# Last expert product of a two-block transformer: activations stationary, 512 table columns streaming

## The chip, the cores and the metric

One Trainium2 chip, one of its cores. The metric is the time of one execution on the device in microseconds (us); the kernel before took 1345.21 us, the median of three runs (1343.98 to 1345.67).

## The reference, cut to what matters

Two transformer blocks run one after the other on 256 tokens of width 1024, in float32. Only the end of the second block is touched:

```python
gate2 = (silu(c) @ w_ada + b_ada)[5 * 1024:]          # one value per channel
h2 = rms_norm(x, g_norm2) * (1 + scale2) + shift2
# peer: 8 heads pick 16 of 16384 experts each, per token
act = gelu(einsum('td,tkd->tk', h2, expert_u[idx]))
y = einsum('tk,tkd->td', g * act, expert_v[idx])       # expert_v: 16384 x 1024
out = x + gate2 * y
```

The kernel does not gather. It multiplies with all 16384 rows of both tables and uses a dense matrix X (16384 experts by 256 tokens) that is zero where an expert was not picked. The last product is y = X^T V, with V = `expert_v`: 256 x 16384 times 16384 x 1024.

## The kernel before, in words

**Products in three passes.** Float32 values are cut in two fp32r parts, high and low (`hilo`, L389: ScalarE copies the high part, VectorE subtracts to get the low part). `mm3` (L262) makes one product of three matmuls, high by high (L265), high by low (L266), low by high (L267), with the first operand pair stationary in TensorE and the second one streaming. Each matmul carries its own weight load.

**Table units.** All weights come in units of 128 x 1024 floats (512 KB). `Units` (L136) keeps five raw buffers ahead by DMA on SyncE's queue, and cuts a unit two ahead of its use: ScalarE writes `whi` (L127), VectorE writes `wlo` (L170), three buffers each. `units.get()` returns the pair and starts the cut of the unit two further on.

**The stage before.** 128 units of the first expert table are multiplied with the normed activations; the results, masked and weighted, lie in `xs0` (128 x 96 x 256 floats, unit i in column block i) and `xs1` (units 96 to 127).

**The stage of the change** (L1417 to the end). `yacc` is four PSUM banks of 128 x 512 floats (`big4`, L288). For each of 128 units i, `w_cut(i)` (L1387) cuts X(i), 128 experts x 256 tokens, in two fp32r parts `wx`, made two units ahead, in buffers of three units, two buffers. `v_unit(i)` (L1393) then takes the eight blocks of 128 table columns in turn: the table block is stationary, the 256 tokens stream. So one unit has 8 x 3 = 24 matmuls of 256 columns, and the sum lies with the 1024 channels on the partitions: bank n//2 holds blocks n and n+1, 256 tokens each. Beside it, eight rows of `w_ada` (`ad`, 512 KB each) are loaded and reduced on VectorE (L1430): they give gate2 as `mod[:, 40:48]`, channels on the partitions. The residual x was stored to DRAM earlier (`hsave`, L1141, channels on the partitions) and is loaded back to `hx` (L1436).

**The end.** Units 126 and 127 are done block by block, both units for block 0, then for block 1 and so on, so that blocks finish one after the other (L1437 to 1440). For each block one VectorE instruction (L1442) computes yacc * gate2 + hx, and five DMAs store the result, the last two of 128 KB.

**What sets the order.** The text is a program for a framework that plans the order of each engine's queue when the kernel is built: an instruction whose inputs are there in the plan's own clock can be placed ahead of earlier text, instructions earlier in the text go first where several are ready. It sets all semaphores from the reads and writes of tiles; in PSUM two accesses to one bank are put in order even where their columns differ. On the chip every queue runs in its planned order.

**A stage with the other operand order** exists in the kernel: `proj_tok` (L431) has token activations stationary and 512 columns of the cut table unit streaming, 12 matmuls of 512 columns per unit, for `v`, `mv`, `sv` and `mlv`.

Of the kernel before, what the change touches and what calls it, by code (L numbers as in the profile page):

```python
# [8 lines left out]
F32 = mybir.dt.float32  # L9
# [4 lines left out]
AF = mybir.ActivationFunctionType  # L14
OP = mybir.AluOpType
AX = mybir.AxisListType

T = 256
# [89 lines left out]
def body(tc, nc, a, out):  # L108
    ctx = ExitStack()
    with ctx:  # L110
        _body(ctx, tc, nc, a, out)


def _body(ctx, tc, nc, a, out):
    V, S, G, PE = nc.vector, nc.scalar, nc.gpsimd, nc.tensor
    cst = ctx.enter_context(tc.tile_pool(name="cst", bufs=1))
    wp = ctx.enter_context(tc.tile_pool(name="wp", bufs=1))
    xp = ctx.enter_context(tc.tile_pool(name="xp", bufs=1))
# [7 lines left out]
    def act(o, i, f, **k):  # L126
        return S.activation(o, i, f, **k)  # L127

    def load(t, src):
        nc.sync.dma_start(t, src)  # L130
        return t
# [53 lines left out]
    units = Units([a["w"][u] for u in range(NU)] + [a["eu"][i] for i in range(128)] + [a["ev"][i] for i in range(128)])  # L185
# [9 lines left out]
    bada = cst.tile([128, 48], F32, name="bada")  # L195
# [34 lines left out]
    def C(name):  # L230
        if name in made:
            return made[name]
        lo, hi = CN[name]
        return cn[:, lo:hi] if hi <= NC1 else cn2[:, lo - NC1:hi - NC1]

    def P_(name, i=None):
        lo, hi = SM[name]
        return sm[:, lo:hi] if i is None else sm[:, lo + i:lo + i + 1]
# [23 lines left out]
    def mm3(o, w, x, start, stop):  # L262

        (wh, wl), (xh, xl) = w, x
        PE.matmul(o, wh, xh, start=start, stop=False, skip_group_check=True)  # L265
        PE.matmul(o, wh, xl, start=False, stop=False, skip_group_check=True)  # L266
        last[0] = PE.matmul(o, wl, xh, start=False, stop=stop, skip_group_check=True).ins  # L267

    def mm(o, w, x, start, stop):
        return PE.matmul(o, w, x, start=start, stop=stop, skip_group_check=True)  # L270

    def pst(tag, shape, bufs):
        return ps.tile(shape, F32, name=tag, tag=tag, bufs=bufs)
# [4 lines left out]
    def p_ax(shape=(128, 512)):  # L278
        return pst("ax", list(shape), 4)
# [4 lines left out]
    def p_first(i, n=T):  # L284

        return (p_acc() if i % 4 < 2 else p_mm())[:, :n]

    def big4():  # L288
        return [p_acc(), p_acc(), p_mm(), p_mm()]
# [4 lines left out]
    o_ = p_ax()  # L294
# [15 lines left out]
    mod = cst.tile([128, 48], F32, name="mod")  # L310
    mraw = cst.tile([128, 48], F32, name="mraw")
# [38 lines left out]
    def rstd(ssum, r):  # L350

        n = r.shape[-1]
        r0 = mp.tile([128, n], F32, name="r0", bufs=2)
        t = mp.tile([128, n], F32, name="rt", bufs=2)
        act(r0, ssum, AF.Ln, bias=epsc)
        act(r0, r0, AF.Exp, scale=-0.5)
        act(t, r0, AF.Square, scale=math.sqrt(0.5))
        V.scalar_tensor_tensor(t, ssum, EPS, t, op0=OP.add, op1=OP.mult)
        V.scalar_tensor_tensor(r, t, 1.5, r0, op0=OP.subtract, op1=OP.mult, reverse0=True)

    class Norm:
# [14 lines left out]
        def finish(self):  # L376
            p = p_ax((128, T))
            tc.keep_in_program_order(mm(p, C("o1024"), self.acc, True, True))
            self.r = mp.tile([128, T], F32, name="rstd", bufs=2)
            rstd(p, self.r)  # L380
# [40 lines left out]
    def proj_T(kind, i, x, o=None, n=T):  # L421
        w = unit(kind, i)
        o = p_mm()[:, :n] if o is None else o
        for c in range(8):
            s = slice(c * 128, (c + 1) * 128)
            mm3(o, (w[0][:, s], w[1][:, s]), (x[0][:, c], x[1][:, c]), c == 0, c == 7)
            if c == 4:
                tick()
        return o
# [32 lines left out]
    def gate_rows(w, mh, x):  # L462

        o = p_mm()[:, :T]
        m = w.shape[2]
        for c in range(8):
            mm(o[0:m], w[:, c], x[0][:, c], c == 0, False)
            mm(o[0:mh], w[:, c, 0:mh], x[1][:, c], False, c == 7)
        return o
# [133 lines left out]
    o = og[0]  # L603
# [52 lines left out]
    for i in range(4):  # L656
        o = proj_T("q", i, xn)
        NL.add(headnorm(o, C("b64"), [(gq[:, 0:1], qn[:, i])], r=n1.r))
        utick()
        o = proj_T("k", i, xn)  # L660
# [36 lines left out]
    for g in (3, 2, 1, 0):  # L697
        o = proj_T("p", g, xn)
# [98 lines left out]
    for i in range(4):  # L797
        o = proj_T("mq", i, xn, p_first(i))
# [83 lines left out]
    t = b2.tile([128, 128], F32, name="below")  # L882
# [59 lines left out]
    for n in range(8):  # L942
        i = n // 2
        outs = [(None, ks[:, i])] if n % 2 else [(gq[:, 2 + j:3 + j], qs[:, 2 * i + j]) for j in range(2)]
        kind = "sk" if n % 2 else "sq"
        if n < NXA:
            o = proj_T(kind, i, xa, p_first(n, T + 2), n=T + 2)
# [4 lines left out]
            while qo and n >= 1:  # L952
                m, o, outs = qo.pop(0)
# [5 lines left out]
        else:  # L959
            o = proj_T(kind, i, xn)  # L960
# [5 lines left out]
    o = gate_rows(wgi, 36, xn)  # L966
# [57 lines left out]
    for i in range(8):  # L1024
        o = proj_T("ml", i, xn)
        b = cpad[i % 2]
        act(b[:, 4:], o, AF.Copy)
        w = [P_("conv_w", 4 * i + j) for j in range(4)]
# [65 lines left out]
    for i in range(4):  # L1094
        o = proj_T("mlo", i, xn)
# [45 lines left out]
    hsave = dr.tile([128, 8, T], F32, name="hsave")  # L1141
# [7 lines left out]
    xs0 = pp_.tile([128, 96, T], F32, name="xs0")  # L1149
    scr = pp_.tile([128, 8192], F32, name="scr", tag="xs1")  # L1150
    scr_u = scr.bitcast(U32)
    o_ = [0]
# [230 lines left out]
    yacc = None  # L1383
    wsp = {}
    wx = [None]

    def w_cut(i):  # L1387
        if i % 3 == 0:
            wx[0] = pp_.tile([128, 3, 2, T], F32R, name="wx", tag="oh", bufs=2)
        wsp[i] = (wx[0][:, i % 3, 0], wx[0][:, i % 3, 1])  # L1390
        hilo(X(i), *wsp[i])

    def v_unit(i):  # L1393
        w = units.get()
        x = wsp.pop(i)
        for n in range(8):
            s = slice(n * 128, (n + 1) * 128)
            mm3(yacc[n // 2][:, (n % 2) * T:(n % 2 + 1) * T], (w[0][:, s], w[1][:, s]), x,
                i == 0 and n % 2 == 0, False)

    gr_ = [0]
    for i in range(128):
# [14 lines left out]
    yacc = big4()  # L1417
# [2 lines left out]

    ad = xp.tile([128, 2, 1024], F32, name="ad", tag="xl")
    load(ad[:, 0], crep_src)
    for i in range(126):
        w_cut(i + 2)
        if i % 12 == 0 and i < 96:
            load(ad[:, 1], a["ada"][40 + i // 12])
        if i % 12 == 8 and i < 96:
            j = 40 + i // 12
            jk = xp.tile([128, 1024], BF, name="jk", tag="xh", bufs=1)
            V.scalar_tensor_tensor(jk, ad[:, 1], 1.0, ad[:, 0], op0=OP.mult, op1=OP.mult, accum_out=mraw[:, j:j + 1])  # L1430
        v_unit(i)
    V.tensor_tensor(mod[:, 40:48], mraw[:, 40:48], bada[:, 40:48], op=OP.add)
    ws = [units.get() for _ in range(2)]
    xs = [wsp.pop(126 + k) for k in range(2)]
    hx = xp.tile([128, 8, T], F32, name="hx", tag="xh", bufs=1)
    load(hx, hsave)  # L1436
    for n in range(8):  # L1437
        s = slice(n * 128, (n + 1) * 128)
        for k, w in enumerate(ws):
            mm3(yacc[n // 2][:, (n % 2) * T:(n % 2 + 1) * T], (w[0][:, s], w[1][:, s]), xs[k], False, k == 1)  # L1440
    for n in range(8):
        V.scalar_tensor_tensor(hx[:, n], yacc[n // 2][:, (n % 2) * T:(n % 2 + 1) * T], mod[:, 40 + n:41 + n], hx[:, n],  # L1442
                               op0=OP.mult, op1=OP.add)
        if n % 2 and n < 6:
            nc.sync.dma_start(out[:, n - 1:n + 1], hx[:, n - 1:n + 1])
        elif n > 5:
            nc.sync.dma_start(out[:, n:n + 1], hx[:, n:n + 1])

# [98 lines left out]
```

## Time and profile before

| what | value |
|---|---|
| median of 3 runs | 1345.21 us |
| profiled execution | 1344.46 us, span 1342.7 us |
| granted TensorE clock, mean | 0.998 of 2.4 GHz |
| TensorE busy | 1331.0 us, 99% of the span, 10821 matmuls |
| VectorE, ScalarE, GpSimd busy | 1006.3, 771.3, 85.5 us |
| DMA | 251.98 MB, mean 188 GB/s |
| the stage of the change | 970.1 us to the end |

The busy time of a matmul is longer than its distance to the next one, since matmuls overlap in the array; what counts is the distance from start to start. Starts are in us from the start of the span.

### The profile page before, as it was taken

The numbers are of one execution on the slowest core, as the hardware profiler recorded it, in microseconds if no ns is written. First come the engines' busy times: TensorE is split into PE (matmuls) and PEld (weight loads), VectorE is DVE, ScalarE is ACT, GpSimd is POOL, SyncE is SP. The second block draws the span as 40 slices with busy tenths as digits, with TensorE's granted clock in tenths as the row PEclk, the third lists the DMA queues.
The fourth block names the chain that finished last, engine by engine and source line by source line (L and its number), as shares of the span: only waits on it lengthen the run. The fifth ranks groups of instructions, "written<-read, shape, count | busy, mean of one in ns | idle before, by whom it ended". The sixth has DMA issues, their size and how long they took to land.

```text
span 1342.7 us, 27108 instructions
## 1 busy us (share of the span) xinstructions
PE 1331.0 (99%) x10821; PEld 1292.2 (96%) x10821; DVE 1006.3 (75%) x1930; ACT 771.3 (57%) x1430; POOL 85.5 (6%) x71
## 2 busy tenths in 40 slices
PE   9999999999999999999999999999999999999998
PEld 7889899999998899999999999999999999999998
DVE  7977698887798789799978888985576555555554
ACT  8757664444588887544756665554444444444442
POOL 0301010000100001086000000000000000000000
PEclk9999999999999999999999999999999999999999
DMA  7535469988543335655555555546687565565553
GB/s 280 179 109 187 143 201 330 327 301 271 161 139 123 126 109 166 216 181 191 172 180 158 158 158 158 158 157 179 190 288 246 183 188 178 184 185 179 186 187 97
DMA packets 70000, 251.98 MB, mean 188 GB/s; under 512 B 7777, under 2 KB 8689, under 8 KB 69489
## 3 DMA queue, kind: packets, MB, share of 16 engines
q1 hardware_dynamic: 69872, 250.24, 57.7%
q8 instruction: 85, 1.39, 0.4%
q14 instruction: 43, 0.34, 0.1%
HBM read 248.11 MB, written 2.10 MB: 186 GB/s over the span
## 4 chain that ended last, share of the span: by engine, by line
PE 95%; DVE 3%; issue 1%; ACT 0%; DMA 0%; DVEq 0%; SPq 0%; ACTq 0%
PE mm L265 18%; PE mm L266 18%; PE mm L267 18%; PE ax L270 9%; PE acc L266 8%; PE acc L265 8%; PE acc L267 8%; PE ax L267 3%; PE ax L266 3%; PE ax L265 3%; DVE wlo L170 1%; DVE xnl L751 1%; DVE xal L751 1%; DVE h L761 1%; PE mm L270 0%
## 5 line engine op out<-in xcount | busy, mean ns | idle before, releaser
L127 ACT ACTIVATE whi<-raw 128x1024 fp32r<-128x1024 f32 (+1 forms) x415 | 438.0, 1056 | 438.5 <-PE mm L266 323.3
L170 DVE TENSOR_TENSOR wlo<-raw,whi 128x1024 fp32r<-128x1024 f32 x392 | 479.1, 1223 | 263.4 <-ACT whi L127 260.8
L265 PE MATMUL mm<-xnh,whi 128*128 128x256 f32 x1304 | 375.2, 288 | 0.0
L267 PE MATMUL mm<-xnh,wlo 128*128 128x256 f32 x1304 | 369.1, 283 | 0.0
L266 PE MATMUL mm<-xnl,whi 128*128 128x256 f32 x1304 | 369.0, 283 | 0.0
L265 PEld LDWEIGHTS mm<-xnh,whi 128*128 128x128 f32 x1304 | 249.7, 191 | 0.9 <-issue 0.3
L266 PEld LDWEIGHTS mm<-xnl,whi 128*128 128x128 f32 x1304 | 250.0, 192 | 0.5
L267 PEld LDWEIGHTS mm<-xnh,wlo 128*128 128x128 f32 x1304 | 249.8, 192 | 0.1
L265 PE MATMUL mm<-wx,whi 128*128 128x256 f32 x512 | 144.9, 283 | 0.0
L266 PE MATMUL acc<-wx,whi 128*128 128x256 f32 x512 | 144.9, 283 | 0.0
L267 PE MATMUL mm<-wx,wlo 128*128 128x256 f32 x512 | 144.9, 283 | 0.0
L265 PE MATMUL acc<-wx,whi 128*128 128x256 f32 x512 | 144.9, 283 | 0.0
L267 PE MATMUL acc<-wx,wlo 128*128 128x256 f32 x512 | 144.9, 283 | 0.0
L266 PE MATMUL mm<-wx,whi 128*128 128x256 f32 x512 | 144.9, 283 | 0.0
L266 PE MATMUL ax<-xnl,whi 128*128 128x256 f32 x352 | 100.1, 284 | 1.5 <-DVE xnl L751 1.5
L267 PE MATMUL ax<-xnh,wlo 128*128 128x256 f32 x352 | 99.7, 283 | 0.4 <-DVE wlo L170 0.4
L265 PE MATMUL ax<-xnh,whi 128*128 128x256 f32 x352 | 99.7, 283 | 0.0
L267 PEld LDWEIGHTS acc<-wx,wlo 128*128 128x128 f32 x512 | 98.3, 192 | 0.0
L265 PEld LDWEIGHTS acc<-wx,whi 128*128 128x128 f32 x512 | 98.3, 192 | 0.0
L266 PEld LDWEIGHTS acc<-wx,whi 128*128 128x128 f32 x512 | 98.3, 192 | 0.0
L265 PEld LDWEIGHTS mm<-wx,whi 128*128 128x128 f32 x512 | 98.3, 192 | 0.0
L266 PEld LDWEIGHTS mm<-wx,whi 128*128 128x128 f32 x512 | 98.3, 192 | 0.0
(380 smaller groups left out, 2504.2 us busy)
## 6 DMA issues: line engine op xcount, KB each, us to landing
raw<-in_w_dram SPq DMA_DIRECT2D x157, 512.0 KB, 4.2
raw<-in_eu_dram SPq DMA_DIRECT2D x128, 512.0 KB, 3.6
raw<-in_ev_dram SPq DMA_DIRECT2D x128, 512.0 KB, 3.9
ada<-in_ada_dram SPq DMA_DIRECT2D x40, 512.0 KB, 5.0
ad<-in_ada_dram SPq DMA_DIRECT2D x8, 512.0 KB, 4.3
h<-in_xT_dram SPq DMA_DIRECT2D x4, 256.0 KB, 5.1
memT<-in_memT_dram SPq DMA_DIRECT2D x1, 1024.0 KB, 6.3
hsave<-h SPq DMA_DIRECT2D x1, 1024.0 KB
```

The source lines that it names most:

```text
L127: return S.activation(o, i, f, **k)
L170: i = e.tensor_tensor(lo, r, hi.bitcast(F32), op=OP.subtract)
L265: PE.matmul(o, wh, xh, start=start, stop=False, skip_group_check=True)
L266: PE.matmul(o, wh, xl, start=False, stop=False, skip_group_check=True)
L267: last[0] = PE.matmul(o, wl, xh, start=False, stop=stop, skip_group_check=True).ins
L270: return PE.matmul(o, w, x, start=start, stop=stop, skip_group_check=True)
L751: V.scalar_tensor_tensor(x[1][:, c, :T], h[:, c], g[:, c:c + 1], x[0][:, c, :T].bitcast(F32), op0=OP.mult, op1=OP.subtract)
L761: V.tensor_tensor(h[:, c], o[:, n * T:(n + 1) * T], h[:, c], op=OP.add)
```

## The change

The last product swaps its operands. The cut activations `wx` are stationary (128 experts x 128 tokens), 512 columns of the table unit stream. One unit has then 4 x 3 = 12 matmuls of 512 columns; bank b holds tokens 128u to 128u+127 on the partitions (u = b // 2) and channels 512n to 512n+511 (n = b % 2). With tokens on the partitions, three things are added. The residual, stored with channels on the partitions, is loaded earlier into the used-up columns 0 to 7 of `xs0`, turned by 16 TensorE transposes of 128 x 128 (`h_turn`, four calls), and copied by ScalarE to columns 8 to 15. The gate must lie along the free axis in every partition: `g_row` (two calls) makes 8 diagonal matrices on VectorE (identity times gate column) and multiplies a matrix of ones with them (one float32 matmul of 512 columns per call), and ScalarE copies the result to `grow`. The end multiplies with `grow` and adds `hT`: two VectorE instructions in place of one. Bank 3 is finished in two halves of 256 columns. The output tensor changes its layout to tokens on partitions; the host turns it back.

```diff
-    def v_unit(i):
-        w = units.get()
-        x = wsp.pop(i)
-        for n in range(8):
-            s = slice(n * 128, (n + 1) * 128)
-            mm3(yacc[n // 2][:, (n % 2) * T:(n % 2 + 1) * T], (w[0][:, s], w[1][:, s]), x,
-                i == 0 and n % 2 == 0, False)
+    def v_unit(i, parts=range(4), start=False, stop=False, w=None, x=None):
+
+        w = units.get() if w is None else w
+        x = wsp.pop(i) if x is None else x
+        for b in parts:
+            u, n = divmod(b, 2)
+            us, s = slice(128 * u, 128 * u + 128), slice(512 * n, 512 * n + 512)
+            mm3(yacc[b], (x[0][:, us], x[1][:, us]), (w[0][:, s], w[1][:, s]), start, stop)
...
+    hx = xs0[:, 0:8]
+    hT = xs0[:, 8:16].rearrange("p a t -> p (a t)").rearrange("p (u d) -> p u d", u=2)
+    gd = xs0[:, 16:20].rearrange("p a t -> p (a t)").rearrange("p (c n) -> p c n", c=8)
+    grow = xs0[:, 20:24].rearrange("p a t -> p (a t)")
+    ones = xs0[:, 24, 0:128]
+
+    def h_turn(k):
+        u, n = divmod(k, 2)
+        p = p_ax()
+        for c in range(4):
+            PE.transpose(p[:, c * 128:(c + 1) * 128], hx[:, 4 * n + c, u * 128:(u + 1) * 128], C("ident"))
+        act(hT[:, u, n * 512:(n + 1) * 512], p, AF.Copy)
+
+    def g_row(n):
+        for c in range(4 * n, 4 * n + 4):
+            V.tensor_scalar(gd[:, c], C("ident"), mod[:, 40 + c:41 + c], None, op0=OP.mult)
+        p = p_ax()
+        mm(p, ones, gd[:, 4 * n:4 * n + 4].rearrange("p c n -> p (c n)"), True, True)
+        act(grow[:, n * 512:(n + 1) * 512], p, AF.Copy)
+
     for i in range(126):
...
-        v_unit(i)
-    V.tensor_tensor(mod[:, 40:48], mraw[:, 40:48], bada[:, 40:48], op=OP.add)
+        v_unit(i, start=i == 0)
+        if i == 30:
+            load(hx, hsave)
+            G.memset(ones, 1.0)
+        if 40 <= i < 56 and i % 4 == 0:
+            h_turn((i - 40) // 4)
+        if i == 98:
+            V.tensor_tensor(mod[:, 40:48], mraw[:, 40:48], bada[:, 40:48], op=OP.add)
+        if i in (102, 106):
+            g_row((i - 102) // 4)
     ws = [units.get() for _ in range(2)]
     xs = [wsp.pop(126 + k) for k in range(2)]
-    hx = xp.tile([128, 8, T], F32, name="hx", tag="xh", bufs=1)
-    load(hx, hsave)
-    for n in range(8):
-        s = slice(n * 128, (n + 1) * 128)
-        for k, w in enumerate(ws):
-            mm3(yacc[n // 2][:, (n % 2) * T:(n % 2 + 1) * T], (w[0][:, s], w[1][:, s]), xs[k], False, k == 1)
-    for n in range(8):
-        V.scalar_tensor_tensor(hx[:, n], yacc[n // 2][:, (n % 2) * T:(n % 2 + 1) * T], mod[:, 40 + n:41 + n], hx[:, n],
-                               op0=OP.mult, op1=OP.add)
...
+    def finish(b, s):
+        u, n = divmod(b, 2)
+        ds = slice(512 * n + s.start, 512 * n + s.stop)
+        V.tensor_tensor(o_[:, b, s], yacc[b][:, s], grow[:, ds], op=OP.mult)
+        V.tensor_tensor(o_[:, b, s], o_[:, b, s], hT[:, u, ds], op=OP.add)
+        nc.sync.dma_start(out[:, u, ds], o_[:, b, s])
+
+    for b in range(3):
+        for k in range(2):
+            v_unit(126 + k, (b,), stop=k == 1, w=ws[k], x=xs[k])
+        finish(b, slice(0, 512))
+    for s in (slice(0, 256), slice(256, 512)):
+        for k in range(2):
+            mm3(yacc[3][:, s], (xs[k][0][:, 128:], xs[k][1][:, 128:]),
+                (ws[k][0][:, 512 + s.start:512 + s.stop], ws[k][1][:, 512 + s.start:512 + s.stop]), False, k == 1)
+        finish(3, s)
```

## Rows read from the trace of the kernel before

**Rows 1.** The profile's page: the span, busy time by engine.

```profile
span 1342.7 us, 27108 instructions
PE 1331.0 (99%) x10821; PEld 1292.2 (96%) x10821; DVE 1006.3 (75%) x1930; ACT 771.3 (57%) x1430; POOL 85.5 (6%) x71
```

**Rows 2.** Busy time in two stretches: us, busy (count) by engine, clock, DMA.

```profile
970.00:1020.00 50.00, 50.00 (x419) 50.00 (x419) 35.11 (x50) 23.77 (x34) 0.00 (x0) 1.00 0.84 277
1050.00:1100.00 50.00, 50.00 (x419) 50.00 (x418) 27.08 (x36) 22.84 (x33) 0.00 (x0) 1.00 0.59 182
```

**Rows 3.** Waits from 970 to 1333: total us, times, longest.

```profile
ACT whi L127 <- PE mm L266: 191.6, 126, 1.8
DVE wlo L170 <- ACT whi L127: 150.7, 116, 1.7
```

**Rows 4.** Timeline of one table unit: start us, us, engine, line.

```profile
1312.79 0.28 PE L265 MATMUL acc<-wx,whi 128*128 128x256 f32 x1
...
1312.87 1.06 ACT L127 ACTIVATE whi<-raw 128x1024 fp32r<-128x1024 f32 x1 [1.82 <-PE mm L266]
...
1313.96 1.23 DVE L170 TENSOR_TENSOR wlo<-raw,whi 128x1024 fp32r<-128x1024 f32 x1 [1.66 <-ACT whi L127]
...
1315.67 0.28 PE L265 MATMUL acc<-wx,whi 128*128 128x256 f32 x1
```

**Rows 5.** Timeline, 512-column matmuls: 12 steps in `v`, then 12 in `mv`.

```profile
13.93 0.39 PE L265 MATMUL acc<-whi,xnh 128*128 128x512 f32 x1
...
16.65 0.39 PE L265 MATMUL acc<-whi,xnh 128*128 128x512 f32 x1
...
137.09 0.40 PE L265 MATMUL acc<-whi,mnh 128*128 128x512 f32 x1
...
139.90 0.39 PE L265 MATMUL acc<-whi,mnh 128*128 128x512 f32 x1
```

**Rows 6.** Timeline: transposes (L525 to L528), then a float32 product (L270).

```profile
63.69 0.27 PE L525 MATMUL ax<-cn,p 128*128 128x128 f32 x1
...
64.23 0.27 PE L528 MATMUL ax<-cn,p 128*128 128x128 f32 x1
64.34 0.60 PE L270 MATMUL ax<-sqacc,o 128*128 128x256 f32 x2
...
64.90 0.28 PE L266 MATMUL mm<-xnl,whi 128*128 128x256 f32 x1
```

**Rows 7.** Two groups of VectorE instructions: busy us, mean ns.

```profile
L842 DVE TENSOR_TENSOR sgu<-ax,rstd 128x512 f32<-128x512 f32 x22 | 15.1, 688 | 7.2 <-PE ax L267 7.1
L391 DVE TENSOR_TENSOR wx<-xs,wx 128x256 fp32r<-128x256 f32 x128 | 46.4, 417 | 0.0
```

**Rows 8.** Instructions of L1432 and L1430, and of tile hx: counts, starts.

```profile
L1432 DVE TENSOR_TENSOR mod<-mraw,bada x1: 159/159/159, 1018.9 to 1018.9; 128x8 f32<-128x8 f32 x1
L1430 DVE SCALAR_TENSOR_TENSOR jk<-ad x8: 1216/1226/1228, 977.6 to 1016.6; 128x1024 bf16<-128x1024 f32 x8
L130 SPq DMA_DIRECT2D hx<-hsave x1: 327/327/327, 1017.9 to 1017.9; - x1
DMA to landing us min/median/max: 2.1/3.1/6.6
```

**Rows 9.** Tile raw, 970 to 1030, its landings.

```profile
DMA to landing us min/median/max: 3.5/4.6/7.0
```

**Rows 10.** Timeline of the end: blocks 0 and 1, and the last block.

```profile
1334.27 0.28 PE L267 MATMUL acc<-wx,wlo 128*128 128x256 f32 x1
...
1334.59 0.87 DVE L1442 SCALAR_TENSOR_TENSOR hx<-acc,mod,hx 128x256 f32<-128x256 f32 x2 [2.13 <-PE acc L267]
...
1338.59 0.28 PE L267 MATMUL mm<-wx,wlo 128*128 128x256 f32 x1
1338.91 0.88 DVE L1442 SCALAR_TENSOR_TENSOR hx<-mm,mod,hx 128x256 f32<-128x256 f32 x2 [0.56 <-PE mm L267]
1339.42 0.81 SPq L1447 DMA_DIRECT2D out_dram<-hx  x2
```

More of the change, by code (lines that the diff above doesn't have):

```diff
@@ L1430, in _body @@
             V.scalar_tensor_tensor(jk, ad[:, 1], 1.0, ad[:, 0], op0=OP.mult, op1=OP.mult, accum_out=mraw[:, j:j + 1])
-        v_unit(i)
-    V.tensor_tensor(mod[:, 40:48], mraw[:, 40:48], bada[:, 40:48], op=OP.add)
+        v_unit(i, start=i == 0)
[8 more added lines that the diff above has]
+            g_row((i - 102) // 4)
     ws = [units.get() for _ in range(2)]
     xs = [wsp.pop(126 + k) for k in range(2)]
-    hx = xp.tile([128, 8, T], F32, name="hx", tag="xh", bufs=1)
-    load(hx, hsave)
-    for n in range(8):
-        s = slice(n * 128, (n + 1) * 128)
-        for k, w in enumerate(ws):
-            mm3(yacc[n // 2][:, (n % 2) * T:(n % 2 + 1) * T], (w[0][:, s], w[1][:, s]), xs[k], False, k == 1)
-    for n in range(8):
-        V.scalar_tensor_tensor(hx[:, n], yacc[n // 2][:, (n % 2) * T:(n % 2 + 1) * T], mod[:, 40 + n:41 + n], hx[:, n],
-                               op0=OP.mult, op1=OP.add)
[L1444 to L1447, printed above, removed]
+    o_ = xs0[:, 32:40].rearrange("p a t -> p (a t)").rearrange("p (b d) -> p b d", b=4)
+    def finish(b, s):
[13 more added lines that the diff above has]
+        finish(3, s)
 def _cols(w, n0):
@@ L1542 @@
         aps[n] = nc.dram_tensor(f"in_{n}_dram", v.shape, mybir.dt.from_np(v.dtype), kind="ExternalInput").ap()
-    out = nc.dram_tensor("out_dram", (128, 8, T), F32, kind="ExternalOutput").ap()
+    out = nc.dram_tensor("out_dram", (128, 2, 1024), F32, kind="ExternalOutput").ap()
     with tile.TileContext(nc) as tc:
@@ L1547 @@
     o = r.results[0]["out_dram"]
-    return np.ascontiguousarray(o.transpose(2, 1, 0).reshape(1, T, 1024))
+    return np.ascontiguousarray(o.transpose(1, 0, 2).reshape(1, T, 1024))
```

## The prediction

> **What bounds the kernel now.** The page first [rows 1]: TensorE is busy for 99% of the span, VectorE for 75%, ScalarE for 57%. A busy TensorE proves little, because matmuls overlap, so I look next at the stage of the change by itself. There TensorE has no hole at all: 50.00 us busy in 50, at the full clock (2.4 GHz), with DMA at 0.84 of its time in the first 50 us and 0.59 later [rows 2]. The waits say the same from the other side: ScalarE waits for TensorE 126 times (whi waits for the last reader of its buffer), VectorE waits for ScalarE, and no row has TensorE waiting [rows 3]. So the stage lasts as long as TensorE needs for its matmuls, from start to start. One unit runs from 1312.79 to 1315.67 [rows 4]: 2.88 us for 24 matmuls, 0.120 us each. At 2.4 GHz 256 columns alone are 0.1067 us; some 13 ns per matmul come on top.
>
> **The change part by part.**
>
> *The operand swap.* A unit has 12 matmuls of 512 columns in place of 24 of 256. The same columns stream, so the gain lies only in what comes on top of them. The kernel already runs this form in `proj_tok`: twelve steps from 13.93 to 16.65 are 2.72 us, 0.2267 us each [rows 5], and 512 columns alone are 0.2133, so again some 13 ns on top. The count is halved and the extra is not doubled: 2.88 - 2.72 = 0.16 us per unit, for 126 units 20.2 us. There is a worse row: in `mv` twelve steps take 137.09 to 139.90 = 2.81 us, 0.234 each, which would leave 0.07 per unit, 8.8 us. I take 0.2267, since the `v` rows come from a long unbroken run over unit borders, beside the same cuts on ScalarE and VectorE, and the changed stage is the longest unbroken run of all; `mv` goes in bursts of some 15 matmuls. I keep 0.234 for the range. The half as many weight loads give nothing more than that: a load is hidden in either row.
>
> The Trainium skill speaks against this gain ("TensorE: Matmul & The Clock Gate", section "Back-to-back issue gap"): the isolated gap is N/2.4 + 2.5 ns, which would be an estimated 109.2 and 215.8 ns here, and the swap would save 31 ns per unit, 3.9 us in all, less than what is added below. The trace has 120.0 and 226.7 ns, so by the rows the extra is five times larger, and with it the gain.
>
> *What must keep up with the shorter unit.* The cut of a unit starts 0.08 us after a unit's start (1312.87) and ends at 1313.96 + 1.23 = 1315.19, 2.4 us after it [rows 4]; it is for a unit two further on, that is 5.44 us after with the new length. 3.0 us of slack stay. ScalarE's and VectorE's work per 50 us is 22.8 and 27.1 us [rows 2]; a unit 6% shorter does not fill them. Raw data: five buffers, so 5 x 2.72 = 13.6 us per turn; less the 2.4 us of the cut some 11 us are left for a landing of 7.0 at worst [rows 9]. At 512 KB per 2.72 us DMA moves 193 GB/s, and the trace has 277 [rows 2]. Cost nothing; were a landing late by its worst 7.0 us, the slack of 3.0 us would leave 4 us per event.
>
> *Residual and gate, in the middle of the stage.* The 16 transposes stand in TensorE's queue. From 63.69 to 64.23 five steps take 0.54 us, 0.108 each [rows 6]: 1.7 us. The two gate products are plain float32; such a product of 256 columns runs as two passes, and from 64.34 to 64.90, less 0.12 us for the fp32r matmul in between, it takes 0.44 us [rows 6]. For 512 columns I double it: 0.88, 1.8 us for both. As bounds, 0.23 each if it ran like the fp32r rows (1.3 less), and twice 0.88 above (1.8 more). After each of six interruptions some matmuls may start at `mv`'s spacing (7 ns more); ten each make 0.4 us, I take 0.3.
> The load of the residual (1 MB), the memset, the new column of `mod`, 8 diagonal products and 6 ScalarE copies leave TensorE's path if the queues put them early. They will: `mod` stood after the loop in the text and ran at 1018.9, right after the last reduction (1016.6), 320 us ahead of its use, and the residual's load ran at 1017.9 [rows 8]. So when TensorE comes to `g_row` the diagonals have long been made, and I cost that wait at nothing. In text order VectorE would do four diagonals (each between the 159 ns of `mod` and the 417 of 256 columns [rows 7, 8]) behind a wlo, and TensorE with all the units behind it would stand for up to 1.1 us, twice. The load is moved past SyncE's queue of raw loads: it takes up to 6.6 us to land [rows 8], as it did before in the same stretch, and no wait came of it [rows 3]. If the first transpose is placed before the landing, TensorE stands up to 6.6 us; if the new uses of `xs0` make ScalarE's cut of `wx` wait for the load, 6.6 - 3.0 = 3.6 us are seen. I take 0 for both, because 30 and 40 units of text lie between, and keep 6.6 for the range.
>
> *The end.* I count from the start of units 126 and 127. Before: the last of 48 matmuls starts at 47 x 0.12 = 5.64, VectorE comes 0.32 later and needs 0.88 for the two blocks of the bank [rows 10], so 6.84 us to the last store's issue. The first bank is read at 1334.59, 0.32 after the last matmul of its second block (1334.27), though its first block was done six matmuls earlier: a bank is read only when all its matmuls are done. After: six matmuls per bank, last starts at 1.13, 2.49, 3.85; VectorE is ready 0.43 later (0.32 and 0.11 for the longer matmul). A finish is two instructions of 512 columns, 0.688 each [rows 7], 1.38 us, a little more than the 1.36 that TensorE needs per bank: VectorE is busy 1.56 to 5.70 without a break. Half A of bank 3 has its last matmul at 4.7, but its product waits for VectorE: 5.70 to 6.12. Half B lies in the same bank, so TensorE stands from 4.8 to some 6.2; its last matmul starts at 6.8, VectorE comes at 7.14 and takes 2 x 0.417: 7.97. The store is of 128 KB as before. Cost 1.1 us. Bounds: 0.3 gain if no bank wait and no backlog existed (24 x 0.2267 = 5.44 against 5.76), 2.0 cost if each handover took 0.3 us more.
>
> *The sum*: -20.2 + 1.7 + 1.8 + 0.3 + 1.1 = -15.3 us. The profiled execution took 1344.46 us (span 1342.7), which gives 1329.2; it lies 0.75 under the median of 1345.21. Against the median: 1329.9 us.
>
> **The rivals.** 0.2%, 2.7 us, is about what a measurement can tell from no change.
>
> *A. The 512-column matmul stays at `mv`'s spacing.* 8.8 gained, 4.9 paid: 1341.3 us. For it: in `mv` it held over whole bursts; against it: 12 matmuls in 2.72 us in `v` [rows 5].
>
> *B. The new work is placed where TensorE meets it.* Load not landed (6.6), or both diagonals late (2.2), on top of the forecast: 1332 to 1337 us. Against it: everything that could go early in the old trace did [rows 8].
>
> *C. Slower: the extra per matmul grows with the width.* Place: all 126 units. At 0.240 us, twice 0.120, nothing is gained and 4.9 us are paid: 1350.1 us. It decides from (2.88 - 4.9/126)/12 = 0.2368 us on. For it: `mv` at 0.234 has gone more than half the way from 0.2267 to 0.240, and is 3 ns short of the break-even; against it, the `v` rows. The skill's isolated gaps above would end on the same side, an estimated 1346.
>
> *D. No change to be told*, some A with some B: 1343 to 1347.
>
> **How the numbers follow.** Forecast with its own uncertain sizes (1327 to 1333): 0.76. A: 0.09. B: 0.07. C: 0.04. D: 0.04. Faster: 0.76 + 0.09 + 0.07 = 0.92; same 0.04; slower 0.04. Below, the bounds give an end with 0.3 gained in place of 1.1 paid and gate products 1.3 cheaper, 2.7 us under the forecast: 1327. Above, the range takes in B up to a stall of 6 us and the part of A that settles half-way: 1336. Outside lie some 0.15.
>
> **What would show it.** In the changed profile one unit lasts 2.72 us, 12 matmuls 0.227 apart; 2.76 or more says A or C. The stage lasts some 353 us where it lasted 369, and what comes before it is as long as now. The 16 transposes and two gate products fill 3.5 us of TensorE, without a wait for VectorE or DMA in front of them; a wait there is B. The copies' ScalarE time and the diagonals cause no wait of TensorE. At the end TensorE waits about 1.4 us for VectorE between the two halves of the last bank, and VectorE runs through the first three finishes without a break. The forecast is wrong if the units' spacing is over 0.230, if a hole of over 1 us stands in the stage before its end, or if the stages ahead of it change length by over 2 us.

## The result and the profile after

The changed kernel takes 1329.19 us (median of four runs, 1329.14 to 1330.08), the kernel before 1344.99 on the same chip (1343.98 to 1345.67): a ratio of 0.9885, 95% interval 0.9868 to 0.9902. That is 15.8 us less. Forecast were 15.3 less and 1329.9 us, with a range of 1327 to 1336. The profiled execution took 1329.14 us with a span of 1327.4, at a mean granted clock of 0.998.

The page of after, against [rows 1]: TensorE still fills 99% of a shorter span, with 1510 matmuls fewer, and its weight loads fall from 96 to 91%.

```profile
span 1327.4 us, 24145 instructions
PE 1313.2 (99%) x9311; PEld 1212.8 (91%) x9311; DVE 1010.4 (76%) x1940; ACT 775.0 (58%) x1436; POOL 85.7 (6%) x72
```

The two stretches of [rows 2] after the change (us, busy time and count of each engine, clock, DMA share, GB/s):

```profile
970.00:1020.00 50.00, 50.00 (x225) 41.52 (x224) 35.67 (x50) 24.15 (x35) 0.00 (x0) 1.00 0.85 297
1050.00:1100.00 50.00, 50.00 (x226) 41.38 (x225) 28.10 (x36) 25.66 (x39) 0.00 (x0) 1.00 0.57 190
```

TensorE is busy throughout at the full clock, as before, and now loads weights for 41.5 us of 50 where it loaded for 50.0. The other engines have the same work and the same room.

The waits from 970 to 1327, against [rows 3] (total us, times, longest):

```profile
...
ACT whi L127 <- PE mm L267: 170.6, 125, 2.1
DVE wlo L170 <- ACT whi L127: 132.5, 114, 2.4
...
DVE xs L1471 <- PE acc L267: 1.8, 1, 1.8
...
PE mm L265 <- DVE xs L1471: 0.5, 1, 0.5
```

ScalarE and VectorE still wait for TensorE. TensorE itself waits once, 0.5 us, and that is at the end.

A table unit after the change, from the timeline of TensorE (start us, us, engine, line), against [rows 4, 5]:

```profile
1199.74 0.39 PE L265 MATMUL mm<-whi,wx 128*128 128x512 f32 x1
...
1202.46 0.39 PE L265 MATMUL mm<-whi,wx 128*128 128x512 f32 x1
```

Twelve steps lie between the two rows: 2.72 us, 0.2267 each. From the start of its first `wx` matmul to that of its last, the stage takes 352.67 us (970.64 to 1323.32) where it took 368.52 (970.07 to 1338.59), and 4.04 us follow to the end of the span where 4.10 followed: together 15.91 less. Two more profiles of the changed kernel gave 352.67 and 352.67. What lies ahead of the stage is not touched, and its length differs from run to run (968.7 to 971.4 over all the runs shown here); so lengths of this stage are compared below beside the times.

### The profile page after: what moved, and what is told of

The parts are those of the page before. It is cut to its first block, busy times and chain, and to the rows that moved or that the text cites. A ratio compares the mean times of both kernels' runs of the same rounds, so it can differ in the third digit from the quotient of the medians.

```text
span 1327.4 us, 24145 instructions
## 1 busy us (share of the span) xinstructions
PE 1313.2 (99%) x9311; PEld 1212.8 (91%) x9311; DVE 1010.4 (76%) x1940; ACT 775.0 (58%) x1436; POOL 85.7 (6%) x72
## 4 chain that ended last, share of the span: by engine, by line
PE 95%; DVE 3%; issue 1%; DMA 1%; ACT 0%; SPq 0%; ACTq 0%; DVEq 0%
PE mm L265 18%; PE mm L266 18%; PE mm L267 18%; PE ax L270 9%; PE acc L266 7%; PE acc L265 7%; PE acc L267 7%; PE ax L267 3%; PE ax L266 3%; PE ax L265 3%; DVE wlo L170 1%; DVE xnl L751 1%; DVE xal L751 1%; DVE h L761 1%; DMA raw<-in_w_dram 1%
## 5 line engine op out<-in xcount | busy, mean ns | idle before, releaser
L267 PE MATMUL mm<-xnh,wlo 128*128 128x256 f32 x1304 | 369.1, 283 | 0.0
L267 PEld LDWEIGHTS mm<-xnh,wlo 128*128 128x128 f32 x1304 | 249.8, 192 | 0.1
L265 PE MATMUL acc<-whi,wx 128*128 128x512 f32 x256 | 100.8, 394 | 0.0
L265 PE MATMUL mm<-whi,wx 128*128 128x512 f32 (+1 forms) x258 | 100.1, 388 | 0.5 <-DVE xs L1471 0.5
L267 PE MATMUL ax<-xnh,wlo 128*128 128x256 f32 x352 | 99.7, 283 | 0.4 <-DVE wlo L170 0.4
L267 PE MATMUL mm<-whi,wx 128*128 128x512 f32 (+1 forms) x258 | 100.0, 387 | 0.0
L266 PE MATMUL mm<-wlo,wx 128*128 128x512 f32 (+1 forms) x258 | 100.0, 387 | 0.0
L267 PE MATMUL acc<-whi,wx 128*128 128x512 f32 x256 | 99.7, 389 | 0.0
L266 PE MATMUL acc<-wlo,wx 128*128 128x512 f32 x256 | 99.6, 389 | 0.0
L266 PEld LDWEIGHTS ax<-xnl,whi 128*128 128x128 f32 x352 | 67.4, 192 | 2.6 <-DVE xnl L751 2.5
L267 PEld LDWEIGHTS ax<-xnh,wlo 128*128 128x128 f32 x352 | 67.5, 192 | 0.6 <-DVE wlo L170 0.6
L265 PEld LDWEIGHTS ax<-xnh,whi 128*128 128x128 f32 x352 | 67.5, 192 | 0.0
L265 PEld LDWEIGHTS mm<-whi,wx 128*128 128x128 f32 x258 | 48.4, 188 | 10.7 <-DVE xs L1471 0.7
L266 PEld LDWEIGHTS mm<-wlo,wx 128*128 128x128 f32 x258 | 48.4, 188 | 10.0
```

## The experiments

"Stage" is the length just defined. The column of differences compares it with the 352.67 of the changed kernel, which three profiles gave. The stage is that of the one profiled execution. The time is a median, except for e2, e3, e4, e6 and e7, which were run once. e1 to e4 ran on a chip where the kernel before took 1345.73 us.

| run | what | time, us | stage, us | difference |
|---|---|---|---|---|
| after | the change | 1329.19 | 352.67 | |
| r_after, r_after2 | the same again | 1328.99, 1329.06 | 352.67, 352.67 | 0 |
| e1_swap256 | swapped, 256 columns | 1348.91 | 372.69 | +20.02 |
| e2_swap128 | swapped, 128 columns | 2158.93 | | |
| e3_no_extra | no turning, no gate products | 1325.57 | 348.91 | -3.76 |
| e4_whole_bank | last bank not split | 1328.77 | 351.72 | -0.95 |
| e5_gate_dma | gate through DRAM | 1329.09 | 352.13 | -0.54 |
| e6_late_diag | diagonals late | 1329.58 | 353.36 | +0.69 |
| e7_late_load | residual's load late | 1329.49 | 353.22 | +0.55 |
| e8_no_pe | turning and gate off TensorE | 1326.81 | 349.60 | -3.07 |
| e9_spread | e8, its transfers spread | 1326.34 | 355.12 | +2.45 |
| e10_rows | e9, gate stored as rows | 1325.96 | 349.07 | -3.60 |

### e1_swap256: the operand order or the width?

The operands stay swapped, but each matmul streams 256 columns.

```diff
-            mm3(yacc[b], (x[0][:, us], x[1][:, us]), (w[0][:, s], w[1][:, s]), start, stop)
+            for q in range(2):
+                qs, ws_ = slice(256 * q, 256 * q + 256), slice(512 * n + 256 * q, 512 * n + 256 * q + 256)
+                mm3(yacc[b][:, qs], (x[0][:, us], x[1][:, us]), (w[0][:, ws_], w[1][:, ws_]), start and q == 0, stop)
```

> The operands stay swapped (activations stationary, table columns streaming), but each unit streams 24 times 256 columns in place of 12 times 512. Theory (the gain is the halved number of matmuls, each with some 13 ns on top of its columns, whichever operand is stationary): 0.120 us per matmul, 2.88 per unit, the gain of 20.2 us is gone and the additions stay: about 1349.4 us, slower than before by 4.5. Rival (the gain comes from having the activations stationary, whose four 128 x 128 blocks serve the whole unit, and not from the width): 2.72 us per unit, about 1329.

1348.91 us (1347.36 to 1349.89), ratio to before 1.0022, 95% interval 1.0012 to 1.0031. In the timeline of TensorE three steps take 0.36 us:

```profile
1199.80 0.28 PE L267 MATMUL mm<-whi,wx 128*128 128x256 f32 x1
...
1200.16 0.28 PE L267 MATMUL mm<-whi,wx 128*128 128x256 f32 x1
```

So 0.120 us each, as in [rows 4] with the other operand order. The stage is 20.02 us longer than with 512 columns. So the theory holds: the gain lies in the width, and with it in half as many matmuls and weight loads. Which operand is stationary makes no difference at 256 columns, and without the width the change is a loss of 0.2%.

### e2_swap128: what comes on top at 128 columns?

As e1, with four matmuls of 128 columns.

> As the changed kernel, but 48 matmuls of 128 columns per unit. Theory in its plain form (13.4 ns on top of 128 columns at 2.4 GHz, 53.3 ns): 0.0667 us each, 3.20 per unit, 126 x 0.48 = 60 us more than the changed kernel, about 1390. Rival (the weight load of a 128 x 128 fp32r block can't be hidden under fewer than some 256 columns, so that a floor near the 0.108 us of the 128-column transposes in the trace of before sets the spacing): 48 x 0.108 = 5.2 us per unit, 310 us more, about 1640.

2158.93 us, far from either number. Ahead of its first stall, in the timeline of TensorE, seven steps take 0.78 us:

```profile
979.84 0.28 PE L266 MATMUL mm<-wlo,wx 128*128 128x128 f32 x1
...
980.62 0.27 PE L267 MATMUL mm<-whi,wx 128*128 128x128 f32 x1
```

That is 0.111 us, 58 ns above the 53 of the columns; at 256 and at 512 it was 13. So a second limit holds at 128 columns, just under the 0.120 of 256. This is the rival's spacing (0.108) and not the theory's (0.067); that the weight load sets it, as the rival has it, the run does not show. At 0.111 a unit needs 5.3 us. The rest of the time is in the busy time by stretch (same columns as above):

```profile
960.00:985.00 25.00, 25.00 (x220) 25.00 (x219) 11.06 (x15) 8.06 (x12) 0.00 (x0) 1.00 0.54 188
985.00:1012.00 27.00, 20.09 (x127) 19.77 (x126) 9.94 (x17) 4.09 (x6) 0.00 (x0) 0.70 0.49 162
1012.00:1050.00 38.00, 38.00 (x180) 38.00 (x180) 8.21 (x11) 4.09 (x6) 0.00 (x0) 0.50 0.31 106
1050.00:1377.00 327.00, 327.00 (x1535) 327.00 (x1535) 51.83 (x73) 43.91 (x65) 0.21 (x1) 0.50 0.16 52
...
2050.00:2150.00 100.00, 100.00 (x898) 100.00 (x898) 28.29 (x35) 22.29 (x31) 0.00 (x0) 1.00 0.21 71
```

TensorE waited 6.9 us of the 27 from 985 on (for `wlo`, up to 4.1 us at a time), the granted clock fell to 0.50 (1.2 GHz), and it stayed there until about 2020 us although TensorE was busy without a break from 1012 on. At 0.50 a matmul takes 327/1535 = 0.213 us, twice 0.107. The timeline of TensorE before and at the rise:

```profile
2015.68 0.41 PE L267 MATMUL mm<-whi,wx 128*128 128x128 f32 x1
2015.89 2.02 PE L270 MATMUL ax<-xs 128*128 128x512 f32 x2
2016.92 1.09 PE L265 MATMUL acc<-whi,wx 128*128 128x128 f32 x1
...
2019.30 0.40 PE L267 MATMUL acc<-whi,wx 128*128 128x128 f32 x1
2019.52 0.30 PE L265 MATMUL acc<-whi,wx 128*128 128x128 f32 x1
2019.66 0.27 PE L266 MATMUL acc<-wlo,wx 128*128 128x128 f32 x1
```

The run answers its question by the rows at full clock alone; the total says nothing of the change.

### e3_no_extra: the price of the added work on TensorE

```diff
-        p = p_ax()
-        for c in range(4):
-            PE.transpose(p[:, c * 128:(c + 1) * 128], hx[:, 4 * n + c, u * 128:(u + 1) * 128], C("ident"))
-        act(hT[:, u, n * 512:(n + 1) * 512], p, AF.Copy)
+        act(hT[:, u, n * 512:(n + 1) * 512].rearrange("p (c t) -> p c t", c=4), hx[:, 4 * n:4 * n + 4, u * 128:(u + 1) * 128], AF.Copy)
...
-        p = p_ax()
-        mm(p, ones, gd[:, 4 * n:4 * n + 4].rearrange("p c n -> p (c n)"), True, True)
-        act(grow[:, n * 512:(n + 1) * 512], p, AF.Copy)
+        act(grow[:, n * 512:(n + 1) * 512], gd[:, 4 * n:4 * n + 4].rearrange("p c n -> p (c n)"), AF.Copy)
```

> The 16 transposes and the two gate products are left out (ScalarE copies the unturned residual and the diagonals in their place, so the output lacks the right residual and gate). Theory: TensorE saves 1.77 and 1.73 us, which no other work hides: 3.5 us less than the changed kernel, about 1325.7. Rival (they stood beside a limit elsewhere, the cut or the DMA): about 1329.

1325.57 us, stage 3.76 us shorter, close to the theory's 3.5. The timeline of after shows the parts, first one call of `h_turn`, then one of `g_row`:

```profile
1081.96 0.39 PE L267 MATMUL mm<-whi,wx 128*128 128x512 f32 x1
1082.20 0.60 PE L1436 MATMUL ax<-cn,xs 128*128 128x128 f32 x4
...
1083.10 0.40 PE L267 MATMUL acc<-whi,wx 128*128 128x512 f32 x1
...
1252.55 0.39 PE L267 MATMUL mm<-whi,wx 128*128 128x512 f32 x1
1252.78 1.02 PE L270 MATMUL ax<-xs 128*128 128x512 f32 x2
...
1254.11 0.40 PE L267 MATMUL acc<-whi,wx 128*128 128x512 f32 x1
```

Each pair of L267 rows is three matmuls apart, 0.68 us if nothing lay between. The first pair has 1.14: 0.44 for four transposes (0.109 each) and some 20 ns of restart. The second has 1.56: a little under 0.88 for the two passes of the float32 product. Times four and two: 1.8 and 1.7 us, and the rest of the 3.76, 0.2 to 0.3, goes in the main to the matmuls after the interruptions, some of which start up to 9 ns wider apart than 227.

### e4_whole_bank: is the split of the last bank worth its stall?

```diff
-    for b in range(3):
+    for b in range(4):
...
-    for s in (slice(0, 256), slice(256, 512)):
...
-        finish(3, s)
```

> The last bank is finished as one piece of 512 columns, not in two halves: no matmul waits for the read of its bank. Theory (the split costs TensorE a stall of 0.7 us, and gives back a shorter last product and a store of half the size): VectorE ends some 0.3 us earlier, the last store is of 256 KB and lands some 1 us later than one of 128 KB: 0.7 us more, about 1329.9, hard to tell from the changed kernel in the time, plain in the trace. Rival (the split only costs): 0.7 us less, about 1328.5.

1328.77 us. The stage is 0.95 us shorter, since TensorE no longer stops, but 5.09 us follow it where 4.04 did, because the last product, addition and store are twice as large: 356.81 against 356.71 in all. By this sum the two expectations (0.7 us more, 0.7 us less) missed by 0.6 and 0.8 us. The split costs as much as it gives.

### r_after, e5_gate_dma, e7_late_load, e8_no_pe

These four ran on one chip. The first is the changed kernel again, 1328.99 us (ratio to before 0.9879, interval 0.9863 to 0.9896).

> The changed kernel once more, beside the two next ones on the same chip: 1329.2 us as before, ratio 0.988 to 0.989.

e5_gate_dma brings the gate to all partitions through DRAM instead of by diagonals and TensorE:

```diff
-        for c in range(4 * n, 4 * n + 4):
-            V.tensor_scalar(gd[:, c], C("ident"), mod[:, 40 + c:41 + c], None, op0=OP.mult)
...
+        if n == 0:
+            gsave = dr.tile([8, 128], F32, name="gsave")
+            nc.sync.dma_start(gsave.rearrange("a b -> b a"), mod[:, 40:48])
+            load(grow, gsave.rearrange("a b -> (a b)")[None, :].to_broadcast([128, 1024]))
```

> The gate row goes through DRAM: one store of 128 x 8 values in turned order and one load that repeats the 1024 values in all partitions, in place of the diagonals, the ones and the two float32 products. Theory (TensorE's time is the stage's time, DMA and SyncE have room): 1.73 us less than the changed kernel, about 1327.4. Rival (the store of single values, 1024 of 4 bytes, or the load of 512 KB delays a raw table unit beyond the 3 us of slack): no gain or some us more, with a wait of ScalarE for DMA in the trace.

1329.09 us (1328.52 to 1329.46), ratio 0.988, interval 0.9864 to 0.9897: nothing gained, as the rival had it. The two products are gone (1.7 us), but the stage is only 0.54 us shorter. Its waits from 990 to 1320 show why:

```profile
ACT whi L127 <- DMA raw<-in_ev_dram: 7.3, 2, 5.9
```

So do its landings of `raw` there, from issue to landing:

```profile
DMA to landing us min/median/max: 3.3/3.5/13.8
```

In after no ScalarE row names a DMA, and the worst landing of that stretch is 5.2. Two matmuls of TensorE start 1.26 us apart at 1038.56, some 1.0 more than the rule. The queue of SyncE shows the store of the gate at 1022.38, one raw load at 1023.52 and the next only at 1032.93, behind the gate's load at 1032.52, which had to wait for the store. Two causes were possible here: the wait in the queue, or the store itself.

e7_late_load holds the residual's load back to unit 40 of the text, close to its use:

```diff
-            load(hx, hsave)
...
+        if i == 40:
+            with tc.issue_after(last_load[0]):
+                load(hx, hsave)
```

> The residual's load is held back in SyncE's queue behind the raw load that stands last in the text at unit 40, and the first turn follows the same unit: the cover of the early load is taken away. Theory (TensorE's queue is planned with a guess of the landing; if the guess is early, TensorE stands for the rest): a hole of 1 to 5 us in front of the first transposes, and as much on the time, 1330 to 1334. Rival (the plan moves the transposes far enough back): no hole, 1329.2.

1329.49 us, stage 0.55 us longer. The first transpose waits for the load:

```profile
1083.29 0.63 PE L1436 MATMUL ax<-cn,xs 128*128 128x128 f32 x4 [0.31 <-DMA xs<-hsave]
```

The load was issued at 1076.7 (982.1 in after) and took 6.5 us, and TensorE came to the transpose some 6 us after the issue, because the plan also moved the transpose back by four matmuls. Neither expectation holds: there is a hole, but the theory's 1 to 5 us were too many. A late landing costs only what exceeds the time between issue and use.

e8_no_pe takes both jobs off TensorE: VectorE transposes blocks of 32 x 32, 16 DMAs of 64 KB move the blocks between partitions, and the gate goes as in e5.

```diff
+    def h_turn(u):
+        V.transpose(tb[:, :, u], hx[:, :, u * 128:(u + 1) * 128].rearrange("p c (a i) -> p a c i", a=4))
+
+    def h_move():
+        for b in range(4):
+            for k in range(4):
+                nc.sync.dma_start(hB[32 * k:32 * k + 32, b], tb[32 * b:32 * b + 32, k])
```

> As the kernel with the gate through DRAM, and the residual is turned without TensorE: VectorE turns 32 x 32 blocks (two instructions of 1024 columns), 16 DMAs of 64 KB inside SBUF move the blocks to their partitions, and the last addition reads them in permuted order. Theory: TensorE has only the products left, 3.5 us less than the changed kernel, about 1325.7. Rival (the reads in runs of 32 columns make the last additions slower on VectorE, or 16 more DMAs in SyncE's queue delay the raw units): less than 2 us gained.

1326.81 us (1324.55 to 1327.33), ratio 0.9864, interval 0.9847 to 0.988, 2.2 us under r_after. The stage is 3.07 us shorter: less than the theory's 3.5, more than the rival's 2. A hole of some 0.6 us at 1069.4 remains, and again the waits have ScalarE waiting for raw data, whose worst landing is 13.8 us:

```profile
ACT whi L127 <- DMA raw<-in_ev_dram: 9.6, 5, 3.4
```

Three of these five waits, 6.2 us together, come at 1064 to 1069, after the gate's store (issued at 1048.5). The other two, at 1026 and 1032, fall among the 16 moves (1008 to 1035) and cost TensorE nothing.

### e6_late_diag, r_after2, e9_spread

These three ran on another chip, where the changed kernel took 1329.06 us (ratio 0.9878, interval 0.9862 to 0.9895).

> The changed kernel beside the next one on the same chip: 1329.1 us.

e6_late_diag holds the eight diagonal products back to their place in the text:

```diff
-            V.tensor_scalar(gd[:, c], C("ident"), mod[:, 40 + c:41 + c], None, op0=OP.mult)
+            with tc.issue_after(units.lo_cut):
+                V.tensor_scalar(gd[:, c], C("ident"), mod[:, 40 + c:41 + c], None, op0=OP.mult)
```

> The eight diagonals of the gate are held in VectorE's queue behind the wlo cut that stands ahead of them in the text, in place of some 80 units early; the plan moves the first product back by two matmuls. Theory (the cover of the early diagonals gone, TensorE stands behind wlo and four diagonals of 0.28 us): a hole of up to 1 us in front of each product, up to 2 us on the time, 1329.5 to 1331. Rival (the two matmuls by which the plan moves the product are enough): no hole, 1329.1.

1329.58 us, stage 0.69 us longer. TensorE reaches the product 0.28 us before it can start (0.51 us between these rows where 0.23 is the rule), twice:

```profile
1252.76 0.39 PE L266 MATMUL acc<-wlo,wx 128*128 128x512 f32 x1
1253.27 1.10 PE L270 MATMUL ax<-xs 128*128 128x512 f32 x2
```

The direction of rival B holds, at a quarter of its price: the plan put the product two matmuls later, which hid most of the diagonals.

e9_spread is e8 with the moves one per two units and the gate's load held back by many units, so that nothing in SyncE's queue waits for the gate's store:

```diff
+        with tc.issue_after(last_load[0]):
+            nc.sync.dma_start(hB[32 * g:32 * g + 32, b], tb[32 * b:32 * b + 32, g])
...
+            with tc.issue_after(last_load[0]):
+                load(grow, gsave[0].rearrange("a b -> (a b)")[None, :].to_broadcast([128, 1024]))
```

> Residual and gate without TensorE as in the kernel before this one, but the load of the gate row stands in SyncE's queue some 25 units behind its store, and the 16 block moves one to every second unit, so that no raw load is queued behind a wait. Theory (the hole of 0.67 us came from raw loads queued behind the wait for the gate's store, not from the bytes): no ScalarE wait for a raw landing, no hole, the stage 3.7 us shorter than in the changed kernel (348.9), about 1325.4 us. Rival (the small packets themselves delay the raw loads): the hole stays or moves.

1326.34 us (median of 1332.26, 1326.48, 1325.76 and 1326.19), ratio 0.9855, interval 0.9839 to 0.9872, 2.7 us under r_after2. The profile is of the 1332.26 run, and it has a large hole; the other three runs, some 6 us faster, can't have had one of that cost, and they were not profiled. The stage of 355.12 is therefore not typical of this kernel. First the landings of the gate's two transfers, the store (issued at 1024.1) and the load (1262.9):

```profile
DMA to landing us min/median/max: 5.9/9.2/12.4
```

The DMA throughput from 1020 to 1075, in 40 slices of 1.4 us:

```profile
GB/s 316 319 331 98 6 0 21 42 27 21 27 48 298 369 423 417 212 304 217 286 286 60 140 241 60 316 60 316 42 331 101 301 83 310 74 307 57 328 72 307
```

And the timeline of TensorE, with the idle time and what ended it in brackets:

```profile
1038.64 0.39 PE L267 MATMUL mm<-whi,wx 128*128 128x512 f32 x1
1041.05 0.50 PE L265 MATMUL acc<-whi,wx 128*128 128x512 f32 x1 [2.02 <-ACT whi L127]
1042.31 0.80 PE L266 MATMUL acc<-wlo,wx 128*128 128x512 f32 x1 [0.76 <-DVE wlo L170]
1042.90 0.63 PE L267 MATMUL acc<-whi,wx 128*128 128x512 f32 x1
```

From 1.4 us after the store's issue on, all 16 DMA engines together moved 0 to 48 GB/s for some 11 us, where the stage needs 193. The store is 4 KB, as 1024 values of 4 bytes; five raw loads of 512 KB were issued in that time. The packets from 1025 to 1026, then from 1026 to 1036:

```profile
DMA packets 1015, 0.00 MB, mean 4 GB/s; under 512 B 1015, under 2 KB 1015, under 8 KB 1015
DMA packets 54, 0.22 MB, mean 22 GB/s; under 512 B 0, under 2 KB 0, under 8 KB 54
```

So the small packets stand in the trace within about 1 us, and the raw loads' packets come sparsely until the store lands, at 1036.5. The wait in the queue is gone and the hole has stayed, so the theory falls: the store itself holds up the raw loads. By what means, the trace does not show.

### e10_rows: the gate stored as eight rows

One TensorE transpose of the gate's 128 x 8 values, a ScalarE copy, and a store of 8 rows of 512 bytes; all else as in e9.

```diff
-            nc.sync.dma_start(gsave[0].rearrange("a b -> b a"), mod[:, 40:48])
+            p = p_ax()
+            PE.transpose(p[0:8, 0:128], mod[:, 40:48], C("ident"))
+            act(xs0[0:8, 28, 0:128], p[0:8, 0:128], AF.Copy)
+            nc.sync.dma_start(gsave[0], xs0[0:8, 28, 0:128])
```

> The residual is turned on VectorE and moved by 16 DMAs spread over 32 units, as in the run before; the gate's column is turned by one TensorE transpose of 128 x 8, copied by ScalarE and stored as 8 rows of 512 bytes instead of 1024 values of 4 bytes. Theory: the 1024 small packets of that store alone delayed the raw loads to 14 us; with 8 rows no raw landing in the stage is over 8 us, ScalarE waits for raw under 1 us in all, TensorE's stage has no hole over 0.3 us, its length is 349.0 to 349.4 (352.67 less 3.5 for the transposes and gate products, plus 0.1 for the one transpose), and the time is 1325.4 to 1325.8, 3.3 under the changed kernel on the same chip. Rival: the 16 moves between partitions or the 512 KB broadcast load delay the raw loads; then a hole stands at 1058 to 1160 or at 1250 to 1290, and the time is 1326.3 or more.

1325.96 us (1324.71 to 1326.88), ratio 0.9856, interval 0.984 to 0.9872. The stage is 349.07 us, within the theory's 349.0 to 349.4; the time is 0.2 above its 1325.4 to 1325.8. From 990 to 1320 the waits have one row for ScalarE:

```profile
ACT whi L127 <- PE mm L267: 160.9, 119, 1.7
```

The landings of `raw` in that stretch:

```profile
DMA to landing us min/median/max: 3.3/3.5/5.5
```

No raw load is late, and TensorE has no hole but the one of the last bank. 349.07 is 0.16 above e3's 348.91: some 0.12 for the one transpose, the rest in the matmuls after it. The store now also runs later, at 1252.5, in place of 1024.1; that this is not the reason is borne out by e8, whose store ran at 1048.5, after the stage's busiest stretch, and was followed by landings of up to 13.8 us. By whole times e8, e9 and e10 can't be told apart (their intervals overlap); by the stage of the profiled runs e10 is the shortest. It beats the kernel before by 19.0 us on one chip. The changed kernel was not run on that chip. Against its two repeats the ratio to before is 0.22 to 0.23% lower (0.9856; 0.9878 and 0.9879), with intervals that overlap; its stage is 3.60 us shorter, and its slowest run, 1326.88 us, lies under the fastest of the changed kernel, 1328.37, on another chip.

## Why the prediction was right

*The bound.* The stage was taken to last as long as TensorE's matmuls from start to start. After the change it is so again: 50.00 us busy in 50, no wait of TensorE before the last bank.

*The swap, -20.2 us.* The forecast spacing was 0.2267 us, from the `v` rows; after shows 2.72 us per unit. e1 takes the width alone back and pays 20.02 us. Rival A (0.234) and rival C (0.240) are out: in the changed stage matmuls start wider apart than 0.230 only for some nine matmuls at its start and after each interruption. The prediction set `mv` [rows 5] aside because it goes in short bursts. That was the right choice, but the reason is only half borne out: in `mv` all 15 or 16 matmuls of a burst start 0.229 to 0.238 apart up to the last, where `v` and the changed stage had settled after ten at most. What else holds `mv` back, no run tells.

The Trainium skill's formula that spoke against the gain ("TensorE: Matmul & The Clock Gate", section "Back-to-back issue gap", N/2.4 + 2.5 ns for an isolated matmul) does not fit this stream of weight loads and matmuls: by it the changed matmul is an estimated 215.8 ns, and the trace has 226.7. The measurement decides, and 13 ns on top at either width are what made the swap pay. What these 13 ns are made of, and so whether a weight load is hidden in either row, as the prediction took it, no run tells.

*The added work on TensorE, +1.7, +1.8 and +0.3.* Measured 1.8, 1.7 and 0.2 to 0.3; e3, without all three, is 3.76 us shorter against 3.8 forecast.

*What was costed at nothing.* The load of the residual, the new `mod` and the diagonals left TensorE's path, as `mod` and the load had done before [rows 8]. Of after, count, durations (min/median/max ns) and starts:

```profile
L1461 DVE TENSOR_TENSOR mod<-mraw,bada x1: 166/166/166, 1022.0 to 1022.0; 128x8 f32<-128x8 f32 x1
L1441 DVE TENSOR_SCALAR xs<-cn,mod x8: 278/279/286, 1022.2 to 1026.9; 128x128 f32<-128x128 f32 x8
L130 SPq DMA_DIRECT2D xs<-hsave x1: 326/326/326, 982.1 to 982.1; - x1
```

The load went out about 100 us before the first transpose (1082.2), the diagonals were done 225 us before the first product (1252.8), though the text puts them 30 and 102 units into the stage. So rival B did not come. e6 and e7 make it come, and it costs 0.7 and 0.6 us, not 2.2 and 6.6: the price was an upper bound. The raw landings stayed at 6.1 at worst in 970 to 1030, against 7.0 in [rows 9].

*The end, +1.1 us: the one term that was mis-sized.* Measured is 0.5: from the start of units 126 and 127 to the last store's issue, 7.36 us (1317.15 to 1324.51) against 6.84 [rows 10]. The timeline of after, VectorE and TensorE around the last bank:

```profile
1317.15 0.39 PE L265 MATMUL acc<-whi,wx 128*128 128x512 f32 x1
...
1321.43 1.13 DVE L1471 TENSOR_TENSOR xs<-mm,xs 128x512 f32<-128x512 f32 x2
...
1321.82 0.28 PE L267 MATMUL mm<-whi,wx 128*128 128x256 f32 x1
...
1322.48 1.02 DVE L1472 TENSOR_TENSOR xs<-xs 128x512 f32<-128x512 f32 x2
1322.62 0.39 PE L265 MATMUL mm<-whi,wx 128*128 128x256 f32 x1 [0.52 <-DVE xs L1471]
...
1324.09 0.42 DVE L1472 TENSOR_TENSOR xs<-xs 128x256 f32<-128x256 f32 x1
```

The working had VectorE go in the order of the text: product and addition of bank 2, then the product of half A, and TensorE behind it 1.4 us. The plan took both products first (L1471 twice, then L1472 twice). Bank 3 was released one addition earlier, and its matmuls at 1321.82 and 1322.62 start 0.8 us apart in place of 0.12: a stall of 0.7 us, half of the 1.4. VectorE was busy without a break from 1318.71 to the last half, as forecast.

*The sum.* -20.2 + 1.8 + 1.7 + 0.25 + 0.5 = -15.95, and stage and end are 15.91 shorter. That the profiled executions differ by just the forecast 15.3 is chance: in the profile of after the stage started 0.57 us later (970.64 against 970.07).

## What to carry to other kernels

Where a stage is bound by TensorE and the same columns can stream in fewer, wider matmuls, price the swap by the start-to-start distance of both shapes in the kernel's own trace, taken from a long unbroken run and not from a burst. Of what this swap added, what stands in TensorE's own queue is paid in full, the last finish on VectorE in part, and what the plan could put early cost nothing; where an instruction's place decides a stall, look up the planned order of its queue instead of the order of the text. A layout turn can leave TensorE, but not by a store of single values: collect them into rows first.

## What the runs showed of the hardware that was not expected

- A store of 1024 values of 4 bytes held up the loads behind it: in e9 all DMA engines together moved 0 to 48 GB/s for some 11 us, and 512 KB loads landed after 13.8 to 14.6 us at worst (e5, e8, e9), against 5.5 in e10. The Trainium skill ("DMA: Bandwidth & Descriptors", section "Why small descriptors are slow (HBM only)") gives small packets to HBM a fixed overhead each, 27% at 256 bytes; the direction agrees, but the runs show far more, and that other transfers pay for it, after the small packets themselves have gone out within 1 us (e9).
- A stall of TensorE can be followed by a lower clock. In e9 TensorE had a hole of 2.4 us from start to start (1038.64 to 1041.05); in the next one, of 1.3 us, the granted clock fell, and it was 0.50 (1.2 GHz) from 1042 to 1048, with 0.427 us per matmul, and 1.00 again from 1049 on. In e5 a hole of 1.3 us alone was followed by matmuls 0.24 us apart, at the full clock.
- In e2 the clock fell after a hole of 3.0 us (992.1 to 995.2): it was 0.78 from 995 to 996 and 0.50 from 996 on, and it did not rise again for some 1000 us. From 1012 to 2015 TensorE was busy all the time with 128-column matmuls. Then it ran the first gate product, two matmuls of 512 columns (2015.89 to 2017.81), and the clock rose 1.7 us later. Whether this brought it back, no run tells.
- In e2 matmuls of 128 columns, each with its own weight load, start 0.111 us apart at the full clock and 0.213 at half of it; at 256 columns it is 0.120 at the full clock (e1). Going from 256 to 128 columns saves next to nothing per matmul here.
